# mLSTM: a fixed issue order of state, denominators and h, a shared gate buffer, one store per output block

## The chip, the cores and the metric

The kernel runs on one core of a Trainium2 chip. The engines meant below are TensorE (PE in the profile, its weight loads PEld), VectorE (DVE), ScalarE (ACT), GpSimd (POOL) and SyncE (SP, which issues almost all DMAs of this kernel). Each engine works through its own instructions in a fixed order and waits for the others through semaphores. The metric is the device time of one execution in microseconds; a comparison takes the median of several.

## What is computed

One encoder layer on x of 2048 tokens x 1024 channels. Three token mixers (a bidirectional mLSTM, a neighbourhood attention, a cross-attention into 256 memory tokens) read one normalised input; their outputs are projected, merged by sigmoid gates, projected again, and a squared-ReLU MLP follows. The change touches the mLSTM alone. Cut to one chunk and one direction, it computes:

```
b      = cumsum(lf);  m_t = max(b + m_state, max_s d_log)          # rows, per token and head
s      = (q k^T) * exp(d_log - m_t)                                # causal scores
num    = s v + w_inter * (C q);   den = sum(s) + w_inter * (n q)
h      = num / max(|den|, exp(-m_t))
C_new  = decay * C + sum_s ws * v k^T ;  n_new likewise
...
h_m    = rmsnorm(h_fwd + h_bwd) * sigmoid(o)                       # 4 heads x 128
```

The forward direction goes over the sequence from its start, the backward one from its end.

## The kernel before

Three phases, each with its own PSUM and SBUF pools. Phase 1 computes the input projection block by block (four blocks of 512 tokens) together with the two attentions. Phase 2 runs the mLSTM while TensorE computes merge gates (`late_gates`, L610): dense groups of 24 matmuls, each 128x512, that come from `ch_group`, and that have little to do with the mLSTM. Phase 3 is the merge, the output projection and the MLP. Every dense fp32 product is three matmuls (L234, L235, L236: high x high, high x low, low x high), for which weights are split into a high part (ACT, L178) and a low part (DVE, L179).

**Order.** TensorE's order is the order in which the program is written (`manual_schedule`, L248). On the other engines a scheduler that works ahead of time picks the order from priorities (earlier in the program comes first) and from its own estimate of when each operand is ready; nothing is reordered on the chip.

**Ticks.** `ch_group` calls `tick` after every second k, four times per group, and each call advances `ml_stream` (L640) by one yield. Four ticks are a slot; slots go forward and backward in turn. A chunk (128 tokens, one direction, all four heads) is a generator, `ml_chunk` (L787), that lives for four slots of its direction: ages 0 to 3. The table `when` (L651) says how many steps of which age run in which tick. Tick 3, after the last matmuls of a dense group, holds nearly all of the mLSTM's own matmuls: call it the burst. In each tick the stream also advances `ml_rows` (L740) by one step: the row quantities (cumulative sums and running maxima by `tensor_tensor_scan`, then small transposes) of the next block of four chunks, for both directions. A set of rows has twelve steps; one set is started at slots 3, 11 and 19 each.

**A chunk's steps.** (A) loads: `sk` (scores and k^T that the other direction stored when it came by that chunk, so that the second visit need not compute them; `given`), `qk`, `v1`, `rb`, `wb`. (B) the decay matrix `de` (ACT exp L821, POOL mask L823). (C) transposes of k (PE L833) into a PSUM tile, a copy into `sk` (ACT L835, first visit), `kw` = k weighted (DVE L838), `qw` (POOL L842). (D) scores (PE L853) and `pt` = scores x `de` (DVE L855, or L847 from `sk`), copies into `sk` (ACT L857), its store. (E) load of `hf`, the other direction's h (second visit). (F) numerators and denominators into the pair of PSUM tiles `pn` (PE L869, L872). (G) the state's update (PE L878, DVE L884), the denominators (ACT abs L889, DVE L890, L892), `h` (DVE L895, two instructions, which read `pn`); on a first visit `h` is stored and the chunk ends; on the second `hf` is added (L900), squares are summed (ACT L903), POOL computes the root (L327, L328), and `og`, the output gate, is loaded (L906). (H) `og` x `h` and the normalisation (DVE L909, L910). (I) transposes (PE L914), a high and a low part `hm` (ACT L916, DVE L917) and two stores.

The order of the steps in the burst is `[3, 1, 2, 1, 2, 0]` by age: I, C, F, D, G, A. PSUM in phase 2 has two tiles for the dense groups, two for `pn` (so one chunk's pair at a time) and four called `mx` for all else: k^T takes one, the scores two, the state's update one. `sk`, `og` and `hm` have one SBUF buffer each (`sk` and `og` per direction), `h` two per direction.

Of the kernel before, what the change touches and what calls it, by code (L numbers as in the profile page):

```python
# [3 lines left out]

# [1 line left out]

# [4 lines left out]
F32 = mybir.dt.float32  # L13
F32R = mybir.dt.float32r
BF16 = mybir.dt.bfloat16
AF = mybir.ActivationFunctionType
ALU = mybir.AluOpType
# [6 lines left out]
TB = 512  # L24
# [15 lines left out]
NB = S // TB  # L40
# [42 lines left out]
class Body:  # L83
# [11 lines left out]
    def t(self, tag, shape, bufs, dt=F32):  # L95

        self.n += 1
        return self.p_a.tile(list(shape), dt, name=f"{tag}_{self.n}", tag=tag, bufs=bufs)
# [191 lines left out]
    def scratch(self):  # L290
        d = lambda name, shape, dt=F32: self.p_d.tile(shape, dt, name=name)
        self.scr = dict(
            qk=d("s_qk", [128, 4, S]),
            v=[d(f"s_v{b}", [TB, 512]) for b in range(NB)],
            og=[d(f"s_o{b}", [TB, 512]) for b in range(NB)],
            gate=[d(f"s_g{b}", [24, 128, TB]) for b in range(NB)],
            qs=d("s_qs", [128, 8, 2, 2, 2, 128]),
            ks=d("s_ks", [128, 2, 2, S]),
            vna=d("s_vna", [2, ROWS, 40, 256]),
            hf=[d(f"s_hf{c}", [128, 512]) for c in range(S // 128)],  # L300
            sk=[d(f"s_sk{c}", [128, 6, 128]) for c in range(S // 128)],
            hna=d("s_hna", [128, 2, 2, S]),
            hmem=d("s_hmem", [128, 2, 2, S]),
            ig=d("s_ig", [8, S]),
            fg=d("s_fg", [8, S]),
            lf=d("s_lf", [8, S]),
            w=[[d(f"s_w{i}{b}", [4, TB]) for b in range(NB)] for i in range(2)],
            r=[[d(f"s_r{i}{b}", [4, 4, 128]) for b in range(NB)] for i in range(2)],
            hm=[d(f"s_hm{b}", [128, 2, 4, TB]) for b in range(NB)],
            hT={b: d(f"s_hT{b}", [128, 2, 8, TB]) for b in SPILL},  # L310
            x2=[d(f"s_x2{b}", [TB, D]) for b in range(NB)],

            a=[[d(f"s_a{i}{q}", [128, 3, 2, TB]) for q in range(FF // 512)] for i in range(NB // 2)],
            s=[[d(f"s_s{i}{q}", [128, 4, 2, TB]) for q in range(FF // 512)] for i in range(NB // 2)],
            t=[d(f"s_t{q}", [128, 2, 2, 2, 512]) for q in range(FF // 512)],
        )
# [321 lines left out]
    def ml_stream(self):  # L640


        rows = self.ml_rows(0)
        for tick in range(START_2):
            if tick >= ROWS_2:
                next(rows, None)
            yield
        slot = 0
        dirs = [list(range(16)), list(range(15, -1, -1))]
        live = [[], []]  # L650
        when = {0: [3, 2], 1: [1], 2: [], 3: [3, 1, 2, 1, 2, 0]}  # L651
        d = 0
        while any(dirs) or any(live[0]) or any(live[1]):
            c = dirs[d].pop(0) if dirs[d] else None

            if slot % 8 == 3 and slot < 24:
                rows = self.ml_rows(slot // 8 + 1)
            slot += 1
            live[d] = [None if c is None else self.ml_chunk(d, c)] + live[d][:3]
            for tick in range(4):  # L660
                for age in when[tick]:
                    if age < len(live[d]) and live[d][age]:
                        next(live[d][age], None)
                next(rows, None)
                yield
            if len(live[d]) == 4:
                live[d][3] = None
            d = 1 - d
# [29 lines left out]
    def ml_consts(self):  # L698
        nc, p = self.nc, self.p_a
        t = lambda name, shape, dt=F32: p.tile(shape, dt, name=name)  # L700


        self.reset = t("reset", [36, TB])
        nc.vector.memset(self.reset, 1.0)
        nc.vector.memset(self.reset.rearrange("p (c t) -> p c t", t=128)[:, :, 0:1], 0.0)
        self.carry = t("carry", [36, 1])
        nc.vector.memset(self.carry, NEG)
        self.pack = [t("r_" + x, [36, TB + 2 * (x == "m")]) for x in "ifbmw"]
        for x in self.pack:
            nc.gpsimd.memset(x, 0.0)  # L710
        self.rows = {}
        self.state = [None, None]

    def row(self, tag, shape, bufs=2):
        self.n += 1
# [24 lines left out]
    def ml_rows(self, n):  # L740
# [35 lines left out]
        for d, b, hs in dirs:  # L776
# [7 lines left out]
            nc.vector.tensor_copy(ac, p[:, :, 4:8])  # L784
            self.rows[d, b] = dict(em=em, ac=ac)

    def ml_chunk(self, d, c):  # L787

        nc = self.nc
        b, cc = c // 4, c % 4  # L790
        cs = slice(cc * 128, cc * 128 + 128)
        first = c == (0 if d == 0 else 15)
        final = c == (15 if d == 0 else 0)
        tl = 127 if d == 0 else 0
# [4 lines left out]
        given = second and (d, c) != (0, 8)  # L799
        gives = not second and (d, c) != (1, 8)  # L800
        sk = self.t(f"sk{d}", [128, 6, 128], 1) if given or gives else None
# [17 lines left out]
        de = self.t(f"de{d}", [128, 4, 128], 1)  # L819
# [8 lines left out]
        if given:  # L828
            pk = sk[:, 4:6]
        elif gives or not final:  # L830
            pk = self.ps("mx")[:, 0:256].rearrange("p (a b) -> p a b", b=128)
            for j in range(2):
                nc.tensor.transpose(pk[:, j], qk[:, 2 + j], self.ident)  # L833
            if gives:
                nc.scalar.activation(sk[:, 4:6], pk, AF.Copy)  # L835
        if not final:
            kw = self.row(f"kw{d}", (128, 4, 64), bufs=2)
            nc.vector.tensor_tensor(kw, pk.rearrange("p a (b e) -> p (a b) e", e=64),  # L838
                                    de[:, :, tl:tl + 1].to_broadcast([128, 4, 64]), ALU.mult)
        if not first:  # L840
            qw = self.row(f"qw{d}", (128, 2, 128), bufs=2)
            nc.gpsimd.tensor_tensor(qw, qk[:, 0:2], wb, ALU.mult)  # L842
        yield
        pt = self.t(f"pt{d}", [128, 4, 128], 1)
        par = lambda x, i: x.rearrange("p (a b) t -> p a b t", b=2)[:, :, i]
        if given:
            nc.vector.tensor_tensor(pt, sk[:, 0:4], de, ALU.mult)  # L847
        else:
            psc = [self.ps("mx", (128, 2, 128)) for _ in range(2)]
            for j in range(2):  # L850
                for i in range(2):
                    hp = slice(i * 64, i * 64 + 64)
                    nc.tensor.matmul(psc[i][:, j], qk[hp, 2 + j], qk[hp, j], start=True, stop=True)  # L853
            for i in range(2):
                nc.vector.tensor_tensor(par(pt, i), psc[i], par(de, i), ALU.mult)  # L855
                if gives:
                    nc.scalar.activation(par(sk[:, 0:4], i), psc[i], AF.Copy)  # L857
# [8 lines left out]
        pn = [self.ps("pn", (128, 2, 129)) for _ in range(2)]  # L866
# [7 lines left out]
        if not final:  # L874
# [10 lines left out]
                                                   pu[:, j], ALU.mult, ALU.add)  # L885
            self.state[d] = Cn
        den = self.small(4, "l")
        for j in range(2):
            nc.scalar.activation(den[:, j::2], pn[j][:, :, 128], AF.Abs)  # L889
        nc.vector.tensor_tensor(den, den, R["em"][:, cc], ALU.max)  # L890
        rec = self.small(4, "l")
        nc.vector.reciprocal(rec, den)  # L892
        h = self.t(f"h{d}", [128, 4, 128], 2)
        for j in range(2):
            nc.vector.tensor_tensor(par(h, j), pn[j][:, :, 0:128],  # L895
                                    rec[:, j::2].unsqueeze(2).to_broadcast([128, 2, 128]), ALU.mult)
        if not second:
            self.store(self.scr["hf"][c], h.rearrange("p a b -> p (a b)"))
            return
# [2 lines left out]
        for i in range(4):  # L902
            nc.scalar.activation(hf[:, i], h[:, i], AF.Square, accum_out=ss[:, i:i + 1])  # L903
        rs = self.rstd(ss, 128, "l", 0.5)
        og = self.t(f"og{d}", [128, 512], 1)
        nc.sync.dma_start(og, self.scr["og"][b][cs])  # L906
        yield
        og = og.rearrange("p (a b) -> p a b", b=128)
        nc.vector.tensor_tensor(og, og, h, ALU.mult)  # L909
        nc.vector.tensor_tensor(h, og, rs.unsqueeze(2).to_broadcast([128, 4, 128]), ALU.mult)  # L910
        yield
        p = self.ps("tr", (128, 4, 128))
        for j in range(4):
            nc.tensor.transpose(p[:, j], h[:, j], self.ident)  # L914
        hm = self.t("hm", [128, 2, 4, 128], 1, F32R)
        nc.scalar.activation(hm[:, 0], p, AF.Copy)  # L916
        nc.vector.tensor_tensor(hm[:, 1], p, hm[:, 0].bitcast(F32), ALU.subtract)  # L917
        for l in range(2):
            self.store(self.scr["hm"][b][:, l, :, cs], hm[:, l].bitcast(F32))
        yield  # L920


# [367 lines left out]
    def load_mix(self, b, mix):  # L1290

        ts = slice(b * TB, (b + 1) * TB)
        for k in range(0, 8, 2):
            for l in range(2):
                if k < 4:
                    src = self.scr["hm"][b][:, l, k:k + 2]
                else:
                    src = self.scr["hna" if k < 6 else "hmem"][:, l, :, ts]
                self.nc.sync.dma_start(mix[l][:, k:k + 2].bitcast(F32), src)
# [306 lines left out]
```

## Time and profile before

| | us |
|---|---|
| median of three runs | 2906.34 (2905.22 to 2908.27) |
| the profiled execution | 2895.78 |
| its span, first to last instruction | 2894.1 |
| TensorE busy in the span | 2859.8 |
| VectorE / ScalarE / GpSimd busy | 2006.1 / 1185.9 / 211.9 |
| granted TensorE clock, mean | 0.999 |

The profile is that of one execution. Its page gives busy times and groups of instructions; its trace can be asked for windows of time, for who waited for whom, for the chain of work that ended last and for the instructions in order of time. In a timeline's row stand the start and the duration, then engine, line, operation, what is written and read, the shape and the count, and in brackets how long the engine had been idle before it and what ended that. [...] The mLSTM lies between about 975 and 1275 us of the span.

### The profile page before, as it was taken

Reading aid. Unit: us, or ns where it says so; the run is one execution under the profiler, and the core shown is the slowest. Engines: PE = TensorE matmul, PEld = TensorE weight load, DVE = VectorE, ACT = ScalarE, POOL = GpSimd, SP = SyncE. Lnnn points to the kernel's source line nnn. Section 1 sums busy time; section 2 is a strip of 40 time slices with the busy share of each in tenths; the row PEclk is TensorE's granted clock in tenths of the full one; section 3 lists DMA queues with packets and bytes.
Section 4 is the critical chain, followed back from the end, with each engine's and each line's share of the span. In section 5 each row is a group of like instructions: output and inputs, shape, how many; then the busy total and the mean of one; then the engine's idle time right before and its main releaser. Section 6 shows DMA issues by size and latency. Waiting matters only on the chain.

```text
span 2894.1 us, 41892 instructions
## 1 busy us (share of the span) xinstructions
PE 2859.8 (99%) x15052; PEld 2364.5 (82%) x15052; DVE 2006.1 (69%) x3438; ACT 1185.9 (41%) x2256; POOL 211.9 (7%) x382
## 2 busy tenths in 40 slices
PE   8999999999999999999999999999999999999999
PEld 6878788878888888788888888888888888888887
DVE  6676865477664455647598887666785988885666
ACT  6465654445543443432243334433322433344331
POOL 4121310021000022310000000000000000000000
PEclk9999999999999999999999999999999999999999
DMA  8786778877999888988444446657863444476654
GB/s 278 229 279 194 241 238 251 263 221 223 287 297 298 264 266 269 288 270 274 120 136 159 157 149 232 229 190 227 300 205 114 142 149 160 150 249 202 195 189 160
DMA packets 345408, 632.78 MB, mean 219 GB/s; under 512 B 29712, under 2 KB 151504, under 8 KB 345200
## 3 DMA queue, kind: packets, MB, share of 16 engines
q1 hardware_dynamic: 345200, 630.10, 67.6%
q8 instruction: 119, 1.95, 0.3%
q14 instruction: 89, 0.73, 0.1%
HBM read 453.37 MB, written 176.62 MB: 218 GB/s over the span
## 4 chain that ended last, share of the span: by engine, by line
PE 79%; issue 8%; DVE 5%; DMA 5%; ACT 1%; SPq 1%; POOL 1%; DVEq 0%; POOLq 0%; ACTq 0%
PE mm L234 25%; PE mm L236 24%; PE mm L235 24%; DVE ws L179 1%; PE tr L1088 1%; DMA sk<-s_sk 1%; DMA wr<-in_w_units_dram 1%; PE pn L869 1%; PE mx L1069 1%; PE mm L1369 0%; PE mx L1102 0%; DVE cy L688 0%; ACT ws L178 0%; PE mx L1241 0%; PE tr L1231 0%
## 5 line engine op out<-in xcount | busy, mean ns | idle before, releaser
L234 PE MATMUL mm<-X,ws 128*128 128x512 f32 x896 | 348.9, 389 | 0.0
L236 PE MATMUL mm<-X,ws 128*128 128x512 f32 x896 | 348.6, 389 | 0.0
L235 PE MATMUL mm<-X,ws 128*128 128x512 f32 x896 | 348.6, 389 | 0.0
L179 DVE TENSOR_TENSOR ws<-wr,ws 128x1024 fp32r<-128x1024 f32 (+1 forms) x194 | 240.1, 1244 | 118.9 <-ACT ws L178 117.9
L234 PE MATMUL mm<-hT,ws 128*128 128x512 f32 (+1 forms) x712 | 283.5, 398 | 1.3 <-ACT ev L564 0.7
L236 PE MATMUL mm<-hT,ws 128*128 128x512 f32 (+1 forms) x712 | 277.0, 389 | 0.0
L235 PE MATMUL mm<-hT,ws 128*128 128x512 f32 (+1 forms) x712 | 276.8, 389 | 0.0
L234 PE MATMUL mm<-ws,hT 128*128 128x512 f32 (+2 forms) x704 | 258.4, 367 | 2.6 <-ACT zif L528 1.9
L178 ACT ACTIVATE ws<-wr 128x1024 fp32r<-128x1024 f32 (+1 forms) x194 | 204.1, 1057 | 122.0 <-PE mm L236 87.4
L236 PE MATMUL mm<-ws,hT 128*128 128x512 f32 (+2 forms) x704 | 249.9, 355 | 2.0 <-DVE hT L437 2.0
L235 PE MATMUL mm<-ws,hT 128*128 128x512 f32 (+2 forms) x704 | 248.7, 353 | 0.0
L236 PE MATMUL mm<-X 128*128 128x512 f32 x616 | 239.7, 389 | 0.1
L234 PE MATMUL mm<-X 128*128 128x512 f32 x616 | 239.6, 389 | 0.0
L235 PE MATMUL mm<-X 128*128 128x512 f32 x616 | 239.6, 389 | 0.0
L204 ACT ACTIVATE ws<-wr 128x512 fp32r<-128x512 f32 x224 | 135.0, 628 | 220.4 <-PE mm L236 139.8
L236 PEld LDWEIGHTS mm<-X,ws 128*128 128x128 f32 x896 | 168.2, 188 | 35.0
L235 PEld LDWEIGHTS mm<-X,ws 128*128 128x128 f32 x896 | 168.2, 188 | 34.8
L234 PEld LDWEIGHTS mm<-X,ws 128*128 128x128 f32 x896 | 168.2, 188 | 34.7
L1491 ACT ACTIVATE X<-X 128x1024 fp32r<-128x1024 f32 x109 | 115.5, 1062 | 197.4 <-DMA X<-s_t 58.8
L1492 DVE TENSOR_TENSOR X<-X 128x1024 fp32r<-128x1024 f32 x109 | 132.6, 1223 | 75.6 <-ACT X L1491 75.2
L1518 DVE TENSOR_TENSOR acc<-acc,mm 128x512 f32<-128x512 f32 x192 | 126.1, 683 | 64.1 <-PE mm L236 64.1
L234 PEld LDWEIGHTS mm<-hT,ws 128*128 128x128 f32 x712 | 134.0, 188 | 29.8 <-issue 4.3
(286 smaller groups left out, 5976.7 us busy)
## 6 DMA issues: line engine op xcount, KB each, us to landing
wr<-in_w_units_dram SPq DMA_DIRECT2D x290, 512.0 KB
s_s<-u SPq DMA_DIRECT2D x32, 1024.0 KB
s_g<-ev SPq DMA_DIRECT2D x96, 256.0 KB
ev<-s_g SPq DMA_DIRECT2D x96, 256.0 KB
s_a<-u SPq DMA_DIRECT2D x96, 256.0 KB
X<-s_s SPq DMA_DIRECT2D x45, 512.0 KB
nab<-in_rpb_dram SPq DMA_DIRECT2D x96, 220.0 KB
xt<-in_w_units_dram SPq DMA_DIRECT2D x32, 512.0 KB
```

The costliest lines, as they stand in the source:

```text
L178: nc.scalar.activation(w[:, 0], raw, AF.Copy)
L179: nc.vector.tensor_tensor(w[:, 1], raw, w[:, 0].bitcast(F32), ALU.subtract)
L204: nc.scalar.activation(hi, src, AF.Copy)
L234: mm(out, lhs[0], rhs[0], start=first, stop=False)
L235: mm(out, lhs[0], rhs[1], start=False, stop=False)
L236: mm(out, lhs[1], rhs[0], start=False, stop=last)
L869: mm(pn[h % 2][:, h // 2], pt[:, h], v1[:, h], start=h < 2, stop=first)
L1069: nc.tensor.matmul(psc[:, :nk], q[:, h, u["half"] * 128:u["half"] * 128 + 128], kl, start=True, stop=True)
L1088: nc.tensor.transpose(ptp[0:120, j], sb[:, j * 120:(j + 1) * 120], self.ident)
L1491: nc.scalar.activation(hi, src, AF.Copy)
L1492: nc.vector.tensor_tensor(lo, src, hi.bitcast(F32), ALU.subtract)
L1518: nc.vector.tensor_tensor(c, c, p, ALU.add)
```

## The change

1. `h` of the step before first: `ml_chunk` keeps, for the chunk that just computed its `h`, the last ACT abs (L889) and the last DVE `h` (L895) in `self.marks`. A new context `behind()` gives each instruction traced in it an edge to the mark on its own engine, so that the scheduler issues it later on that engine. It is an order, not a wait: no semaphore is added.
2. Step C is split: the transposes and `qw` stay; `kw` and the copy of k^T move into a new step with `pt` and the other copies. Step D is split into the scores' matmuls and that new step, which is held `behind()`. Step I is split into the transposes and `hm` with its store, `hm` held `behind()`; in H only the second multiplication is.
3. `when` for tick 3 becomes `[3, 1, 2, 1, 2, 3, 1, 0]`: I's transposes, C's transposes, F, D's scores, G, then `hm`, then `kw` and `pt`, then A. TensorE meets its matmuls in the burst in the same order as before.
4. `ml_rows` advances in ticks 0 to 2 only, three steps a slot in place of four.
5. Buffers: `og` three, shared by both directions (before: one each); `h` one per direction (two); `hm` two (one).
6. `hm` is stored by one DMA in place of two; the DRAM scratch `s_hm` has its axes merged, with the same bytes at the same places, and `load_mix` reads it accordingly.

```diff
-            hm=[d(f"s_hm{b}", [128, 2, 4, TB]) for b in range(NB)],
+            hm=[d(f"s_hm{b}", [128, 8, TB]) for b in range(NB)],
...
-        when = {0: [3, 2], 1: [1], 2: [], 3: [3, 1, 2, 1, 2, 0]}
+        when = {0: [3, 2], 1: [1], 2: [], 3: [3, 1, 2, 1, 2, 3, 1, 0]}
...
-                next(rows, None)
+                if tick < 3:
+                    next(rows, None)
...
+    @contextlib.contextmanager
+    def behind(self):
+
+        with contextlib.ExitStack() as stack:
+            for ins in self.marks:
+                stack.enter_context(self.tc.issue_after(ins))
+            yield
...
-            if gives:
-                nc.scalar.activation(sk[:, 4:6], pk, AF.Copy)
-        if not final:
-            kw = self.row(f"kw{d}", (128, 4, 64), bufs=2)
-            nc.vector.tensor_tensor(kw, pk.rearrange("p a (b e) -> p (a b) e", e=64),
-                                    de[:, :, tl:tl + 1].to_broadcast([128, 4, 64]), ALU.mult)
...
-        if given:
-            nc.vector.tensor_tensor(pt, sk[:, 0:4], de, ALU.mult)
-        else:
+        if not given:
...
-            for i in range(2):
+        yield
+        with self.behind():
+            if gives:
+                nc.scalar.activation(sk[:, 4:6], pk, AF.Copy)
+            if not final:
+                kw = self.row(f"kw{d}", (128, 4, 64), bufs=2)
+                nc.vector.tensor_tensor(kw, pk.rearrange("p a (b e) -> p (a b) e", e=64),
+                                        de[:, :, tl:tl + 1].to_broadcast([128, 4, 64]), ALU.mult)
+            if given:
+                nc.vector.tensor_tensor(pt, sk[:, 0:4], de, ALU.mult)
+            for i in range(2) if not given else ():
                 nc.vector.tensor_tensor(par(pt, i), psc[i], par(de, i), ALU.mult)
                 if gives:
                     nc.scalar.activation(par(sk[:, 0:4], i), psc[i], AF.Copy)
...
-            nc.scalar.activation(den[:, j::2], pn[j][:, :, 128], AF.Abs)
+            marks.append(nc.scalar.activation(den[:, j::2], pn[j][:, :, 128], AF.Abs))
...
-        h = self.t(f"h{d}", [128, 4, 128], 2)
+        h = self.t(f"h{d}", [128, 4, 128], 1)
...
+        self.marks = marks[1].ins, marks[3].ins
...
-        og = self.t(f"og{d}", [128, 512], 1)
+        og = self.t("og", [128, 512], 3)
...
-        nc.vector.tensor_tensor(h, og, rs.unsqueeze(2).to_broadcast([128, 4, 128]), ALU.mult)
+        with self.behind():
+            nc.vector.tensor_tensor(h, og, rs.unsqueeze(2).to_broadcast([128, 4, 128]), ALU.mult)
...
-        hm = self.t("hm", [128, 2, 4, 128], 1, F32R)
-        nc.scalar.activation(hm[:, 0], p, AF.Copy)
-        nc.vector.tensor_tensor(hm[:, 1], p, hm[:, 0].bitcast(F32), ALU.subtract)
-        for l in range(2):
-            self.store(self.scr["hm"][b][:, l, :, cs], hm[:, l].bitcast(F32))
+        yield
+        hm = self.t("hm", [128, 2, 4, 128], 2, F32R)
+        with self.behind():
+            nc.scalar.activation(hm[:, 0], p, AF.Copy)
+            nc.vector.tensor_tensor(hm[:, 1], p, hm[:, 0].bitcast(F32), ALU.subtract)
+        self.store(self.scr["hm"][b][:, :, cs], hm.rearrange("p l h t -> p (l h) t").bitcast(F32))
...
-                    src = self.scr["hm"][b][:, l, k:k + 2]
+                    src = self.scr["hm"][b][:, 4 * l + k:4 * l + k + 2]
```

More of the change, by code (lines that the diff above doesn't have):

```diff
@@ L7 @@
+import contextlib
 import functools
@@ L712, in ml_consts @@
         self.state = [None, None]
+        self.marks = ()
     def row(self, tag, shape, bufs=2):
@@ L887, in ml_chunk @@
         den = self.small(4, "l")
+        marks = []
         for j in range(2):
-            nc.scalar.activation(den[:, j::2], pn[j][:, :, 128], AF.Abs)
+            marks.append(nc.scalar.activation(den[:, j::2], pn[j][:, :, 128], AF.Abs))
         nc.vector.tensor_tensor(den, den, R["em"][:, cc], ALU.max)
@@ L892, in ml_chunk @@
         nc.vector.reciprocal(rec, den)
-        h = self.t(f"h{d}", [128, 4, 128], 2)
+        h = self.t(f"h{d}", [128, 4, 128], 1)
         for j in range(2):
-            nc.vector.tensor_tensor(par(h, j), pn[j][:, :, 0:128],
-                                    rec[:, j::2].unsqueeze(2).to_broadcast([128, 2, 128]), ALU.mult)
+            marks.append(nc.vector.tensor_tensor(par(h, j), pn[j][:, :, 0:128],
+                                                 rec[:, j::2].unsqueeze(2).to_broadcast([128, 2, 128]), ALU.mult))
+        self.marks = marks[1].ins, marks[3].ins
         if not second:
```

## The prediction

> **What bounds the kernel now.** I read the page's engine table first, then the windows over the mLSTM's stretch, then TensorE's waits, then the instructions in order of time around each of them.
>
> ```profile
> span 2894.1 us, 41892 instructions
> PE 2859.8 (99%) x15052; PEld 2364.5 (82%) x15052; DVE 2006.1 (69%) x3438; ACT 1185.9 (41%) x2256; POOL 211.9 (7%) x382
> 975.00:1115.00 140.00, 137.45 (x912) 112.88 (x911) 75.67 (x179) 58.32 (x176) 28.59 (x47) 1.00 0.85 265
> 1115.00:1275.00 160.00, 157.95 (x978) 129.69 (x977) 101.65 (x211) 70.20 (x270) 42.92 (x75) 1.00 0.88 270
> PE pn L869 <- DVE h L895: 2.6, 2, 1.5
> PE pn L869 <- ACT de L821: 2.0, 3, 1.1
> ```
>
> The first two rows are the page's, the next two the windows that hold the whole mLSTM (length, then the busy time of PE, PEld, DVE, ACT, POOL, then clock and DMA), the last two from the list of waits (total, times, longest). TensorE sets the time. In the 300 us that the change touches it is idle for 140.00 - 137.45 = 2.55 us and 160.00 - 157.95 = 2.05 us: 4.60 us together, 0.16% of the run. And all of it stands in one place: 2.6 + 2.0 us ahead of L869, the first matmuls into `pn`. That is the most that the change can win by removing idle time. The rest of TensorE's work in the stretch keeps its number, its order and, at a granted clock of 1.00, its speed.
>
> Now two of the five waits, on TensorE and then on VectorE.
>
> ```profile
> 1054.04 0.38 PE L833 MATMUL mx<-ident,qk 128*128 128x128 f32 x2
> 1055.94 1.13 PE L869 MATMUL pn<-v,pt 128*128 128x129 f32 x8 [1.52 <-DVE h L895]
> ...
> 1220.19 1.02 PE L869 MATMUL pn<-v,pt 128*128 128x129 f32 x7 [1.11 <-ACT de L821]
> ```
>
> ```profile
> 1047.32 1.21 DVE L754 TENSOR_TENSOR_SCAN r_b<-reset,r_f 4x512 f32<-4x512 f32 x1 [5.66 <-DMA r_f<-s_lf]
> 1048.46 1.25 DVE L760 TENSOR_TENSOR_SCAN r_m<-r_f,r_m,r_i 4x512 f32<-4x512 f32 x1
> 1049.64 1.19 DVE L179 TENSOR_TENSOR ws<-wr,ws 128x1024 fp32r<-128x1024 f32 x1
> 1050.75 0.40 DVE L838 TENSOR_TENSOR kw<-mx,de 128x256 f32<-128x256 f32 x1
> 1051.09 0.73 DVE L855 TENSOR_TENSOR pt<-mx,de 128x256 f32<-128x256 f32 x2
> ...
> 1052.44 1.22 DVE L754 TENSOR_TENSOR_SCAN r_b<-reset,r_f 4x512 f32<-4x512 f32 x1
> ...
> 1055.26 0.76 DVE L895 TENSOR_TENSOR h<-pn,sm 128x256 f32<-128x256 f32 x2
> ...
> 1056.20 0.68 DVE L763 TENSOR_TENSOR r_i<-r_i,r_b 36x512 f32<-36x512 f32 x1
> ...
> 1057.63 1.81 DVE L771 TENSOR_TENSOR r_w<-r_b,r_m 4x512 f32<-4x512 f32 x2
> ```
>
> There is one pair of `pn` tiles, so a burst's L869 waits for the `h` of the burst before. Here that `h` ends at 1055.26 + 0.76 = 1056.02, just when L869 starts. Ahead of it VectorE had waited for the row loads until 1047.32, then done two scans, a weight split, `kw`, `pt`, the state and more row work, another scan among it.
>
> ```profile
> 1216.48 0.43 DVE L838 TENSOR_TENSOR kw<-sk,de 128x256 f32<-128x256 f32 x1 [4.05 <-DMA sk<-s_sk]
> 1216.82 0.69 DVE L910 TENSOR_TENSOR h<-og,rs 128x512 f32<-128x512 f32 x1
> ...
> 1218.03 0.80 DVE L847 TENSOR_TENSOR pt<-sk,de 128x512 f32<-128x512 f32 x1
> ...
> 1219.52 0.74 DVE L895 TENSOR_TENSOR h<-pn,sm 128x256 f32<-128x256 f32 x2
> 1218.98 0.64 SPq L803 DMA_DIRECT2D sk<-s_sk  x1
> ```
>
> The longest of the three waits named after `de` is the same wait: `h` ends at 1219.52 + 0.74 = 1220.26, where L869 starts at 1220.19. VectorE stood 4.05 us at a `kw` whose `sk` had not landed, with that `h` behind it. It is a loop: `sk` has one buffer per direction, its next load is issued (SP, last row, 1218.98) when `pt` (to 1218.83) has read it, and the `kw` that waits for such a load stands in VectorE's queue about a slot before its turn in the program, ahead of the `h` of an earlier burst. Of a slot of 8.49 us (below) 4.05 are lost there.
>
> **The change part by part.**
>
> *`h` ahead of `kw`, `pt`, `hm`.* In the second half (three waits, 2.0 us) `kw` can no longer stand ahead of its slot's `h`, so the 4.05 us of waiting for `sk` fall behind it, and the load has two slots to land. I take these 2.0 us as gone. In the first half (two waits, 1.52 us and the rest of 2.6, about 1.0) what leaves the place ahead of `h` is `kw` and `pt`, 0.40 + 0.73 = 1.13 us. The scans and the weight split, on which no edge is put, may stay there. So the shorter wait goes wholly and 1.52 falls to 0.39: 1.0 + 1.13 = 2.1 us gone. Bounds: nothing gained (the scheduler fills the place with another split of 1.19 us) and 2.6 us (the scans move too). I take 2.1, since in the quoted slot `kw` and `pt` are 1.13 of the delay by measurement.
>
> What is late next? Behind `h` now wait `kw` and `pt` for two slots hence, which nobody needs soon, and the PSUM tiles that they read. For that I need a slot's shape.
>
> ```profile
> 1082.63 0.38 PE L833 MATMUL mx<-ident,qk 128*128 128x128 f32 x2
> ...
> 1084.39 0.61 PE L853 MATMUL mx<-qk 64*128 64x128 f32 x8
> ...
> 1085.52 0.50 PE L234 MATMUL mm<-hT,ws 128*128 128x512 f32 x1
> ...
> 1091.12 0.38 PE L833 MATMUL mx<-ident,qk 128*128 128x128 f32 x2
> 1067.22 0.43 PE mm L234
> 1068.68 0.76 DVE L895 TENSOR_TENSOR h<-pn,sm 128x256 f32<-128x256 f32 x2
> 1040.52 0.72 ACT L857 ACTIVATE sk<-mx 128x256 f32<-128x256 f32 x2 [1.29 <-DVE pt L855]
> ```
>
> A burst takes 1085.52 - 1082.63 = 2.89 us, then 5.60 us of dense matmuls follow, and the scores begin 1.76 us into the next burst. A first-half burst takes all four `mx` tiles. The state's is read first and serves the next k^T; the scores' two must be free 5.60 + 1.76 = 7.36 us after the burst. In a slot without row work `h` ends 1068.68 + 0.76 - 1067.22 = 2.22 us after its burst; `kw`, `pt` and half of the last row's copies add 0.40 + 0.73 + 0.36, which makes 3.7 us. 3.6 us of room: cost nothing. ACT's copies wait behind the abs and for `pt`; the dense groups' evacuation behind them has a slot of 8.49 us, so nothing there either.
>
> [...]
>
> *Rows in ticks 0 to 2.* No work goes; a set of twelve steps takes four slots, not three, and is done at the set's fourth slot, two slots before its first user is loaded. TensorE's transposes for the second direction leave the burst for the middle of a dense group.
>
> ```profile
> 1071.15 0.39 PE L236 MATMUL mm<-hT,ws 128*128 128x512 f32 x1
> 1071.47 0.22 PE L781 MATMUL mx<-ident,r_m 4*128 4x4 f32 x1
> ...
> 1072.40 0.40 PE L235 MATMUL mm<-hT,ws 128*128 128x512 f32 x1
> ...
> 1076.47 0.22 PE L781 MATMUL mx<-ident,r_m 4*128 4x4 f32 x1
> ...
> 1077.05 0.50 PE L234 MATMUL mm<-hB,ws 128*128 128x512 f32 x1
> ```
>
> Behind a burst they cost 1077.05 - 1076.47 = 0.58 us. Inside a group, from L236 to L235, 1072.40 - 1071.15 = 1.25 us, where two dense matmuls alone would take 0.46: 0.79 us. That is 0.21 us more, three times: +0.6 us. They need an `mx` tile half a dense stretch, 2.8 us, after the burst, when at least the state's is free; bound 0 to 1 us, I take 0.
>
> *Buffers and stores.*
>
> ```profile
> ACT hm L916 <- DMA s_hm<-hm: 4.6, 4, 1.7
> 1190.81 0.38 SPq L104 DMA_DIRECT2D s_hm<-hm  x1
> SPq L104 <- ACT sk L857: 19.2, 14, 3.9
> 1094.12 5.38 DMA s_g<-ev
> ```
>
> The second `hm` ends four waits of ACT, none of them on TensorE's path: nothing. One store fewer for each of 16 blocks is 16 x 0.38 = 6 us of SP, on which TensorE waits nowhere in this stretch: nothing. One `h` per direction: the first-half `h` must be stored before its direction's next, 17 us later, and a store of this size lands in about 5.4 us (last row, a store of the same 256 KB): nothing; it would cost if SP fell 10 us behind. SP already waits for ACT's copies at the store of `sk` (19.2 us in 14 times); these now come behind `h` and `pt`, about 1 us later, and behind that store stand the loads of the next chunk and of weights. TensorE waits for none of them here, and the chunk's loads have a slot to spare: nothing, against about 1 us in each of 15 slots if that cover went. Three shared `og`: a load comes a slot sooner; nothing.
>
> *Sum*: -2.0 - 2.1 + 0.6 = -3.5 us. On the profiled span 2894.1 becomes 2890.6. The profiled execution took 2895.78 us, 10.6 less than the median of 2906.34; as the change acts on counted microseconds, I take the same 3.5 us from the median: **2902.8 us**, 0.12% down. About 0.2% (5.8 us) is what a measurement of this kernel can tell from no change, so I expect no difference that can be told.
>
> **The rivals.**
>
> *First-half waits stay.* The row scans remain ahead of `h` and a weight split fills the place of `kw` and `pt`. For: splits and scans carry no edge. Against: with `kw` gone, 1.13 us are gone too unless something takes their place. -2.0 + 0.6: 2904.9.
>
> *The change doesn't do what it says.* If the edges only move the wait (the `og` product, which has no edge, waits for its load ahead of `h` as `kw` did for `sk`), the idle time stays and the switching is paid: 2906.9. Against: `og` is loaded more than a slot ahead of its product.
>
> *Slower: the score tiles come free late.* In the row slot above `h` ended at 1056.02; its burst had ended a dense stretch of 5.60 us before 1054.04, so 7.6 us earlier; without `kw` and `pt` it is 6.5. If then `r_i`, `r_b`, `r_w` (1056.20 to 1059.44, 3.2 us) run before `kw` and `pt`, the score tiles are free at 6.5 + 3.2 + 1.5 = 11.2 us, against the 7.36 that decide: TensorE waits 3.8 us at L853. Three sets give +11.4; with the forecast's -3.5 that is +7.9: 2914.2. Against: `kw` and `pt` come earlier in the program than those rows, so that the scheduler prefers them once `h` is issued.
>
> *Faster.*
>
> ```profile
> PE mm L234 <- ACT ev L607: 1.4, 2, 0.7
> ```
>
> All five waits go (4.6), the switching costs nothing, and the waits for ACT's evacuations near the stretch go too (1.4 us by the same list): -6.0, 2900.3.
>
> **How the numbers follow.** Forecast 0.55; first-half waits stay 0.15; no effect 0.07; slower 0.14; faster 0.09. Forecast, first and second rival lie within 0.2%: 0.77, of which I give 0.02 to each side for what the trace cannot show of the scheduler's choices. Faster 0.11, within 0.73, slower 0.16. The range holds forecast and the first two rivals and reaches halfway into the others, whose sizes are bounds: 2899 to 2913.
>
> **What would show it.** Right: no idle before L869 between 975 and 1275 us, or one of 0.4 us in a row slot; `kw` and `pt` behind `h` on VectorE; the 4 us before `kw` on `sk` no longer ahead of `h`; the second direction's small transposes 0.2 us dearer. Wrong: idle time of TensorE before L853 or L833 (score tiles), before L781, or before L234 (evacuations), or a stretch outside phase 2 that moved.

## The result, and the profile after

| | before, us | changed, us |
|---|---|---|
| median of nine runs each on one chip | 2905.22 (2901.48 to 2910.51) | 2894.83 (2890.84 to 2899.52) |
| ratio, 95% interval | | 0.9965 (0.9954 to 0.9976) |
| the profiled execution's span | 2894.1 | 2893.1 |

The change takes 10.4 us off, 0.36%, where the prediction had 3.5 us and "no difference that can be told"; the time lies 4.2 us below the lower end of its range. The first two lines of the changed kernel's page:

```profile
span 2893.1 us, 41875 instructions
PE 2861.0 (99%) x15052; PEld 2364.8 (82%) x15052; DVE 2004.3 (69%) x3438; ACT 1187.3 (41%) x2256; POOL 216.4 (7%) x382
```

The two profiled spans differ by 1.0 us only, while the medians differ by 10.4. So the pair of spans says nothing of the change; where the time went must be read inside the stretch. The windows of the changed kernel over the mLSTM (length, busy time of PE, PEld, DVE, ACT, POOL, clock, DMA share, GB/s):

```profile
975.00:1115.00 140.00, 140.00 (x923) 114.80 (x922) 75.71 (x170) 58.11 (x173) 27.17 (x47) 1.00 0.83 262
1115.00:1275.00 160.00, 160.00 (x989) 131.75 (x988) 99.79 (x220) 73.15 (x277) 47.06 (x77) 1.00 0.88 279
```

TensorE is busy for 140.00 of 140.00 and 160.00 of 160.00 us. The 4.60 us of idle time are gone, all five waits. And VectorE's order of time in the changed kernel, one slot of the second half:

```profile
1205.52 0.58 DVE L897 SCALAR_TENSOR_TENSOR C<-C,wb,mx 128x129 f32<-128x129 f32 x2
1206.02 0.74 DVE L909 TENSOR_TENSOR h<-pn,sm 128x256 f32<-128x256 f32 x2
...
1207.88 0.42 DVE L863 TENSOR_TENSOR kw<-sk,de 128x256 f32<-128x256 f32 x1
1208.21 0.68 DVE L866 TENSOR_TENSOR pt<-sk,de 128x512 f32<-128x512 f32 x1
...
1216.34 0.68 DVE L866 TENSOR_TENSOR pt<-sk,de 128x512 f32<-128x512 f32 x1
```

`kw` and `pt` stand behind `h`, and no bracket stands behind `kw`: it waits for nothing. From one `pt` to the next are 1216.34 - 1208.21 = 8.13 us, TensorE's own pace of about 8.2 us a slot.

The same line before tells what the prediction overlooked. VectorE's `pt` in the kernel before, the first and the last of four in a row:

```profile
1189.71 0.67 DVE L847 TENSOR_TENSOR pt<-sk,de 128x512 f32<-128x512 f32 x1
...
1218.03 0.80 DVE L847 TENSOR_TENSOR pt<-sk,de 128x512 f32<-128x512 f32 x1
```

That is (1218.03 - 1189.71)/3 = 9.44 us a turn. `pt` frees `sk`, the load is issued, `kw` waits for it, and the rest of VectorE's work stands behind `kw` until the next `pt`: the loop of the prediction, but with a period of its own, in these turns some 1.2 us longer than TensorE's slot. Not every turn is that long: from the first `pt` that reads `sk` to the fifteenth, over the 14 turns of the second half, the mean is 8.70 us (1127.38 to 1249.12), against 8.34 us in the changed kernel (1131.89 to 1248.67). A turn that is longer than the slot takes the difference from the lead that VectorE has over TensorE, and TensorE waits only when the lead is used up: here at 1201.40, 1210.61 and 1220.19, at the end of the row of long turns. What one execution shows as idle time is what is left after the lead.

### The profile page after: what moved, and what is told of

Same layout as the page of the kernel before. It is cut to its first block, busy times and chain, and to the rows that moved or that the text cites. A ratio compares the mean times of both kernels' runs of the same rounds, so it can differ in the third digit from the quotient of the medians.

```text
span 2893.1 us, 41875 instructions
## 1 busy us (share of the span) xinstructions
PE 2861.0 (99%) x15052; PEld 2364.8 (82%) x15052; DVE 2004.3 (69%) x3438; ACT 1187.3 (41%) x2256; POOL 216.4 (7%) x382
## 4 chain that ended last, share of the span: by engine, by line
PE 89%; DVE 3%; issue 3%; DMA 3%; ACT 1%; POOL 0%; SPq 0%; DVEq 0%; POOLq 0%; ACTq 0%
PE mm L235 27%; PE mm L237 27%; PE mm L236 27%; PE tr L1105 1%; PE pn L882 1%; PE mx L1086 1%; PE mx L1119 1%; PE pn L885 1%; PE mx L891 1%; DVE ws L180 1%; DMA nav<-s_vna 1%; PE mx L1258 1%; PE tr L1248 1%; DMA xt<-in_xT_dram 0%; DMA wr<-in_w_units_dram 0%
```

## The experiments

Theory A, throughout: the gain is that loop (one `sk` buffer, `kw` on VectorE ahead of `h`), and its price varies with the lead. In the first twelve expectations the other letters stand for rivals that are spelled out there; from the thirteenth on, B, C, C1 and C2 are new theories, of another question. Ratios are to the kernel before, in runs on the same chip.

**1. The kernel before once more** (no edit).

> The kernel before, unchanged, to see an execution of usual length: the one in the profile took 2895.8 us, the median is 2905.2. Theory A (the loop over sk): a transfer that lands later is paid one for one, so the missing 9 us stand before L869 between 975 and 1290 us: 10 us or more of TensorE idle there, most of it after 1130 us. Theory B (row work): the same sum, but between 1040 and 1115 us, at the row sets. Theory D (elsewhere): idle before L869 stays near 4.6 us and the 9 us stand in phase 1 or in the tail. Times: ratio 1.00 for all.

2903.47 us, ratio 0.9988 (0.9978 to 0.9998): two sets of runs of one program differ by 0.1%, just beyond the stated interval, which is the size of error to keep in mind below. Its profile is another execution. TensorE's waits in the stretch, in the first half (first row) and the second (second row):

```profile
PE pn L869 <- DVE h L895: 4.1, 2, 2.5
PE pn L869 <- ACT de L821: 5.6, 6, 1.6
```

These are 9.7 us in eight waits, where the first profile had 4.6 in five, of the same program. VectorE's order of time over a turn, and two loads of `sk` as SP issues them (`SPq` is SP's queue):

```profile
1192.34 0.68 DVE L847 TENSOR_TENSOR pt<-sk,de 128x512 f32<-128x512 f32 x1
...
1194.64 1.00 DVE L900 TENSOR_TENSOR h<-h,hf 128x512 f32<-128x512 f32 x1
1195.68 0.69 DVE L909 TENSOR_TENSOR og<-og,h 128x512 f32<-128x512 f32 x1
1200.64 0.43 DVE L838 TENSOR_TENSOR kw<-sk,de 128x256 f32<-128x256 f32 x1 [4.27 <-DMA sk<-s_sk]
1200.98 0.68 DVE L910 TENSOR_TENSOR h<-og,rs 128x512 f32<-128x512 f32 x1
...
1203.56 0.75 DVE L895 TENSOR_TENSOR h<-pn,sm 128x256 f32<-128x256 f32 x2
```

```profile
1194.42 1.13 SPq L803 DMA_DIRECT2D sk<-s_sk  x1
...
1213.21 0.82 SPq L803 DMA_DIRECT2D sk<-s_sk  x1
```

`pt` ends at 1193.02, the load is issued at 1194.42, `kw` starts at 1200.64, and the `h` of the burst comes 2.92 us behind it. Now the length of the stretch, by the first and the last of the matmuls into `pn` (duration min/median/max in ns, then first and last start), for the kernel before, this run and the changed kernel:

```profile
L869 PE MATMUL pn<-v,pt x256: 271/275/348, 994.3 to 1261.9; 128*128 128x129 f32 x128
```

```profile
L869 PE MATMUL pn<-v,pt x256: 271/275/349, 991.8 to 1265.2; 128*128 128x129 f32 x128
```

```profile
L882 PE MATMUL pn<-v,pt x256: 272/275/277, 998.3 to 1260.6; 128*128 128x129 f32 x128
```

267.6, 273.4 and 262.3 us. Against the first profile the change is worth 5.3 us, against the second 11.1, and the medians say 10.4. Run 4 below, a kernel without the edges that takes as long as the one before, gives a third pair, in which both profiles are of the execution with the median time (2906.65 and 2894.83 us):

```profile
L869 PE MATMUL pn<-v,pt x256: 271/275/552, 997.4 to 1271.6; 128*128 128x129 f32 x128
```

274.2 - 262.3 = 11.9 us, where the two times differ by 11.8. In this pair the whole difference lies inside the stretch. So the execution in which the prediction counted was a short one of its kernel (its 2895.78 us lie below all nine times of before, 2901.48 to 2910.51), and short in this very place.

**2 to 4. One part alone**: the edges with the split of the steps (parts 1 to 3 of the change), the rows in three ticks (part 4), the buffers and the single store (parts 5 and 6), each in the kernel before.

```diff
+        self.marks = marks[1].ins, marks[3].ins
...
+        with self.behind():
```
```diff
-                next(rows, None)
+                if tick < 3:
+                    next(rows, None)
```
```diff
-        h = self.t(f"h{d}", [128, 4, 128], 2)
+        h = self.t(f"h{d}", [128, 4, 128], 1)
...
-        og = self.t(f"og{d}", [128, 512], 1)
+        og = self.t("og", [128, 512], 3)
...
```

> Only the split steps, their order and the edges behind abs and h; rows in all four ticks, buffers and the two stores as before. Theory A: nearly all of the gain, 9 us (ratio 0.997), no idle before L869 after 1130 us. Theory B: 2 to 3 us, since row scans still stand ahead of h in four ticks. Theory C (buffers): 2 us at most, since one og and one hm hold up SP. Theory D: anything within 3 us.

> Only the rows kept off tick 3. Theory A: within 2 us of before; the wait for sk ahead of h stays. Theory B: 7 us or more faster. Theory C and D: within 2 us.

> Only the buffers (og three shared, h one, hm two) and one store of hm. Theory A and B: within 2 us of before. Theory C (SP held up at the og load and the hm stores lets sk's load go late): 7 us or more faster, with kw waiting less than 2 us for sk.

| | us | ratio, 95% interval |
|---|---|---|
| edges alone | 2898.14 | 0.9975 (0.9965 to 0.9985) |
| rows alone | 2903.83 | 0.9998 (0.9989 to 1.0008) |
| buffers and store alone | 2906.65 | 1.0004 (0.9994 to 1.0014) |

The edges, together with the split of the steps, carry most of the gain; the other two are nothing by themselves. With the edges alone no wait before `pn` is left, but a new one has come, in the first half:

```profile
PE mx L783 <- DVE kw L862: 2.1, 2, 1.4
```

L783 are the row work's small transposes. Their tile among the four `mx` is the one that `kw` reads, and `kw` now stands behind `h`. In TensorE's order of time with the edges alone:

```profile
1073.61 0.66 PE L890 MATMUL mx<-v,kw 128*64 128x129 f32 x8
1075.63 0.19 PE L783 MATMUL mx<-ident,r_m 4*128 4x4 f32 x1 [1.36 <-DVE kw L862]
```

Rows in tick 3 put these transposes right behind the burst, where `kw` has just been held back. This is the slower rival's mechanism (what stands behind `h` frees its PSUM late), met by other matmuls than the rival's, and at 2.1 us instead of 11.4 (it is not in the changed kernel, whose rows stay out of tick 3).

**5 and 6. The loop broken without the edges, and the split without the edges.** Five is the kernel before with two `sk` buffers per direction (and one `h`, to make room); six is the changed kernel without its marks, so that `behind()` gives no edge.

```diff
-        sk = self.t(f"sk{d}", [128, 6, 128], 1) if given or gives else None
+        sk = self.t(f"sk{d}", [128, 6, 128], 2) if given or gives else None
...
-        h = self.t(f"h{d}", [128, 4, 128], 2)
+        h = self.t(f"h{d}", [128, 4, 128], 1)
```
```diff
-        self.marks = marks[1].ins, marks[3].ins
```

> The kernel before with two sk buffers per direction (h one per direction, to make room), no edges. Theory A (the loop pt, load of sk, kw through one sk buffer, with kw ahead of h): the load is issued two slots ahead, so no wait of kw for sk over 1 us after 1150 us and no idle before L869 in the second half; the first-half waits stay (2.5 to 4 us): 5 to 7 us faster, ratio about 0.998. Rival A' (VectorE's sheer load ahead of h, not the load of sk): the second-half waits stay, ratio 1.000.

> The kernel after without its edges: split steps, their order, rows in ticks 0 to 2 and all buffers stay. If the edges do it (theory A): kw stands ahead of h again, idle before L869 of 4 us or more, ratio 0.9985 to 1.000. If the order in which the steps are written is enough (rival): ratio 0.9965, as the kernel after.

Five: 2896.05 us, ratio 0.9974 (0.9963 to 0.9985). The second half has no wait before `pn` left; in the first half are 1.5 us before `pn` and 0.9 before the row transposes. VectorE in run 5:

```profile
1188.54 0.68 DVE L847 TENSOR_TENSOR pt<-sk,de 128x512 f32<-128x512 f32 x1
...
1198.58 0.43 DVE L838 TENSOR_TENSOR kw<-sk,de 128x256 f32<-128x256 f32 x1
...
1205.06 0.68 DVE L847 TENSOR_TENSOR pt<-sk,de 128x512 f32<-128x512 f32 x1
```

`kw` waits for nothing, though it still stands ahead of an `h`, and two turns of `pt` take 1205.06 - 1188.54 = 16.52 us, 8.26 each. One buffer more does for the second half what the edges do, with `kw` still early. That is the strongest evidence for theory A: the loop is what was cut, by either means. The gaps of 4.05 us (first profile, before 1216.48) and 4.27 us (run 1, before 1200.64) stand on VectorE, though TensorE is the engine that sets the pace; that they came from too few buffers, run 5 shows.

Six: 2897.26 us, ratio 0.9979 (0.9968 to 0.9990), between what the two expectations had, with 5.2 us of idle time before `pn` in its profile. The order in which the steps are written doesn't move `kw` by itself: it still stands ahead of `h`, and waits.

```profile
1206.90 0.42 DVE L863 TENSOR_TENSOR kw<-sk,de 128x256 f32<-128x256 f32 x1 [1.82 <-DMA sk<-s_sk]
...
1211.51 0.76 DVE L909 TENSOR_TENSOR h<-pn,sm 128x256 f32<-128x256 f32 x2
```

The list of VectorE's waits in the second half of run 6:

```profile
DVE kw L863 <- DMA sk<-s_sk: 22.0, 7, 8.6
```

In the kernel before the same list has 31.5 us in 11 waits. So the split, the rows and the buffers without the edges bring some 6 us of the 10, with the loop still there; which of them does it no run shows, and neither is it shown what the edges would bring without the split.

**9 and 10. Two parts together**: edges and rows with the old buffers and two stores; edges and buffers with the rows in all four ticks.

> Edges and rows in ticks 0 to 2, with the buffers and the two stores of before. If the buffers and the single store are worth nothing: as the kernel after, 9 to 10 us faster than before (ratio 0.9965 to 0.997), with no idle before L869 nor before the rows' small transposes. If they matter once the edges are there (rival: SP's queue is the next limit, since e8 lost 19 us to five more issues a slot): 0.998 or above, with idle before the transposes of h.

> Edges and buffers, rows in all four ticks. If the rows' move only removes the 2.1 us that the edges alone showed before the rows' small transposes (they wait there for kw to free its PSUM tile) and costs 0.6 us: 1.5 us slower than the kernel after, ratio 0.997 to 0.9975, with about 2 us of idle before those transposes. If the move does more (row scans ahead of h): 4 us or more slower than the kernel after.

Nine: 2894.06 us, ratio 0.9960 (0.9948 to 0.9973), which is the whole change's. Ten: 2898.10, ratio 0.9973 (0.9962 to 0.9984), with the same 2.1 us before L783 as the edges alone. So the gain is some 7 us of the edges with the split and another 3 to 4 us for keeping the rows off tick 3 (4.0 us between runs 9 and 10, on one chip), which by itself is worth nothing: it removes a wait that only the edges bring. By the traces that second part is 2.1 us; the rest can't be told from the error of the runs. Buffers and store add nothing that can be measured.

**7, 8, 11, 12. A load of `sk` meant to land later**, in the kernel before and in the changed one: cut into six loads (7, 8), or read in pieces of 256 bytes from a padded scratch (11, 12).

```diff
-            nc.sync.dma_start(sk, self.scr["sk"][c])
+            for j in range(6):
+                nc.sync.dma_start(sk[:, j], self.scr["sk"][c][:, j])
```
```diff
-            sk=[d(f"s_sk{c}", [128, 6, 128]) for c in range(S // 128)],
+            sk=[d(f"s_sk{c}", [128, 12, 80]) for c in range(S // 128)],
...
```

> The kernel before with the load of sk as six DMAs in place of one (same bytes), so that it lands later by five issues of SP, 2 to 3 us. Theory A: the loop runs once a slot on 11 to 13 slots and each turn grows by that: 15 to 30 us slower, all of it before L869 in the second half. Rival A' or D: within 4 us.

> The kernel after with the same six DMAs. Theory A: the load has two slots to land, nothing before L869; as the kernel after, ratio 0.9965 to 0.998. Rival (the load of sk still sets the pace, or SP's issue time does): slower than the kernel after by 10 us or more.

> [...] Theory A (the loop through sk): 5 to 25 us slower, in step with how much later kw starts after the issue, all before L869 in the second half. Rival (only SP's issue time counts): within 3 us of before.

> The kernel after with the same short pieces. Theory A: the load has two slots, so nothing before L882 (pn) in the second half; as the kernel after, ratio 0.9965 to 0.998. Rival: as much slower than the kernel after as e11 is than before.

| | before, us | changed, us |
|---|---|---|
| six loads | 2918.85, 1.0054 (1.0038 to 1.0070) | 2914.16, 1.0043 (1.0028 to 1.0058) |
| pieces of 256 bytes | 2910.84, 1.0016 (1.0007 to 1.0025) | 2927.98, 1.0081 (1.0067 to 1.0095) |

A miss. The changed kernel, in which the load of `sk` has 15 us from issue to `kw`, was to take a slower one for nothing; it lost 19 and 33 us (counted from 0.9965 of the kernel before on the same chip), more than the kernel before (14 and 5). The kernel before lost its time elsewhere than expected, too: mainly at the transposes of `h` (9.6 us with six loads, 10.0 us with short pieces), not before `pn`. TensorE waits there (L931) in the changed kernel with six loads as well:

```profile
DVE h L916 <- DMA hf<-s_hf: 24.4, 9, 4.7
PE tr L931 <- DVE h L927: 16.3, 6, 5.3
```

It is not `sk` that is late, but `hf`, which was not touched.

**13 and 14. Is it `hf` held behind the load of `sk`?** The changed kernel with six loads, and `hf` issued by ScalarE; and edges and rows with six loads and two `sk` buffers.

```diff
-            nc.sync.dma_start(hf, self.scr["hf"][c].rearrange("t (h e) -> t h e", h=4))
+            nc.scalar.dma_start(hf, self.scr["hf"][c].rearrange("t (h e) -> t h e", h=4))
```

> The changed kernel with the load of sk cut into six (as in the run of that name, 2914.16 us), and the load of hf issued by ScalarE instead of SP. Theory B (in the changed kernel the load of hf stands behind the waiting load of sk in SP's queue, the sum h + hf waits for it, and kw and pt stand behind that sum): hf no longer waits for pt, so the waits at h + hf for hf and TensorE's waits at the transposes of h go, and the time falls to 2894 to 2902 us. Theory C (six transfers are dear in themselves, by SP's issue time and the slower landing, whatever stands behind them): the time stays at 2910 to 2916 us.

> The edges and the shifted row work with the buffers of before, the load of sk cut into six, and two sk buffers per direction (one h buffer, to make room). Theory B: the load of sk no longer waits for the pt of the slot before, so nothing is held behind it in SP's queue; TensorE's waits at the transposes go, 2894 to 2902 us. Theory C: SP issues as many transfers as before and each sk lands as late after its issue, so 2910 to 2916 us.

2914.48 (1.0043, 1.0029 to 1.0058) and 2917.22 us (1.0048, 1.0033 to 1.0063). Theory B falls: the loss stayed in both (22 and 25 us, counted in the same way). In 14 VectorE still waits 22.2 us for `hf`. In 13, with `hf` off SP, the wait for it went, as B said, but `og`, the next load in SP's queue, was late in its place:

```profile
DVE og L925 <- DMA og<-s_o: 18.1, 4, 6.7
PE tr L931 <- DVE h L927: 11.3, 5, 4.4
```

**15 and 16. SP's time or the landing of `sk`?** Eight loads of 4 rows of 32 bytes, which nothing reads, behind the one load of `sk`, in the changed kernel and in the one before.

```diff
+            for j in range(8):
+                nc.sync.dma_start(self.t("few", [4, 8], 24), self.scr["qk"][0:4, j % 4, c * 128:c * 128 + 8])
```

> The changed kernel with its one load of sk as it was, and eight loads of 4 rows of 32 bytes behind it on SP, which nothing reads. A small load of SP's takes 0.36 us (r_f from s_lf, 4x512, in the trace of the changed kernel), so SP gets some 2.9 us a slot more to issue, as with five more loads of 64 KB at 0.6 us, while hardly a byte more is moved and sk lands as before. Theory C1 (what cost 19 us is SP's issue time: 0.62 of the stretch plus 2.9 of a slot of 8.25 us is 0.97, so SP falls behind and hf, og and wb are late): 2908 to 2918 us, with waits of TensorE at the transposes of h. Theory C2 (what cost it is the later landing of sk itself): 2893 to 2898 us, no such waits.

> The kernel before with the same eight small loads behind each load of sk. Theory C1: 2910 to 2920 us, waits at the transposes of h, as with sk cut into six (2918.85 us). Theory C2: 2902 to 2908 us, no waits at the transposes.

2942.02 us (1.0139, 1.0124 to 1.0154) and 2935.79 us (1.0113, 1.0096 to 1.0130). No sign of C2, and a loss beyond C1's ranges: some 50 us in the changed kernel (counted as above) and 34 in the one before, for loads that together move 1 KB a chunk. One turn of SP in the changed kernel with the small loads, in order of time (start, duration):

```profile
1209.01 0.67 SPq L814 DMA_DIRECT2D sk<-s_sk  x1
1209.73 5.38 SPq L816 DMA_DIRECT2D few<-s_qk  x8
1215.21 0.39 SPq L819 DMA_DIRECT2D qk<-s_qk  x1
...
1216.96 1.25 SPq L830 DMA_DIRECT2D wb<-s_w  x2
1218.25 0.59 SPq L105 DMA_DIRECT2D s_g<-ev  x1
...
1219.37 0.45 SPq L878 DMA_DIRECT2D hf<-s_hf  x1
1219.86 0.48 SPq L923 DMA_DIRECT2D og<-s_o  x1
1220.44 0.57 SPq L105 DMA_DIRECT2D s_hm<-hm  x1
1221.11 0.81 SPq L814 DMA_DIRECT2D sk<-s_sk  x1
```

A turn of SP takes 1221.11 - 1209.01 = 12.10 us, against TensorE's 8.2, and between the rows stand no more than 0.1 us. But the row of eight runs from the start of the first small load to the end of the last. What one of them took SP (ns, least, median and most of 120), and what SP waited for between them, from 1209 to 1216 us:

```profile
L816 SPq DMA_DIRECT2D few<-s_qk x120: 239/293/1152, 1081.6 to 1281.6; - x120
SPq L816 <- DMA s_hm<-hm: 1.0, 1, 1.0
SPq L816 <- DMA sk<-s_sk: 0.7, 1, 0.7
```

So a small load took 0.29 us at the median, less than the 0.36 us of the expectation, and 1.7 of the 5.38 us are not issuing: SP stood at a small load until a store and a load that it had issued earlier had landed. From 1155 to 1275 us such waits at the small loads add up to 24.8 us; in the changed kernel SP waits for no transfer in that window. Why a load that touches neither tile waits for them isn't shown. Without the 1.7 us the turn would still be 10.4 us, more than TensorE's 8.2. So SP's queue sets the pace, by the time to issue and by these waits together; the runs don't part the two. TensorE waits for it at the transposes:

```profile
PE tr L932 <- DVE h L928: 32.4, 10, 6.2
```

The DMA engines are less busy meanwhile. The hardware queue from 1155 to 1235 us, packets, MB and share of 16 engines, in the changed kernel and then with the small loads:

```profile
q1 hardware_dynamic: 26004, 25.05, 97.7%
```

```profile
q1 hardware_dynamic: 18611, 17.26, 69.9%
```

In the changed kernel itself their packets take nearly all of the time (97.7%); with the small loads more than a quarter of that is free again, and the kernel is slower.

So these runs were no test of theory A. With six loads SP's turn is 12 us too (from 1202.51 to 1214.58 in run 8, with waits for landings in it as well), and with short pieces the load next behind `sk` stays on SP for long; the changed kernel with pieces of 256 bytes, SP in order of time:

```profile
1199.69 0.68 SPq L814 DMA_DIRECT2D sk<-s_sk  x1
1200.46 5.10 SPq L817 DMA_DIRECT2D qk<-s_qk  x1
...
1210.50 0.67 SPq L814 DMA_DIRECT2D sk<-s_sk  x1
```

10.8 us a turn. Why that issue takes 5.10 us instead of 0.4 to 0.6 was not tried apart, and no row shows whether `sk` itself landed later with short pieces; in the kernel before with short pieces the scheduler's order on VectorE differed as well (`kw` at 1204.11, right ahead of its `pt` at 1204.45). Theory A rests on runs 1, 2, 5 and the turns of `pt`, and covers the second half. The waits before `pn` in the first half, where no `kw` reads a loaded `sk`, are the other part of the gain: 2.6, 4.1, 2.4 and 4.6 us in the kernel before, in run 1, 3 and 4, none in run 2. What they stand behind is the prediction's reading (`kw`, `pt` and row work ahead of `h`); no run took that apart.

## Why the prediction was wrong

**The step that failed** is the term of the sum for the second half: "three waits, 2.0 us ... I take these 2.0 us as gone", and with it the sentence that carried the count over, "as the change acts on counted microseconds, I take the same 3.5 us from the median". The mechanism was the one that acted: `sk`'s one buffer, its load, `kw` ahead of `h`, one slot a turn. Only its size was read from the idle time of one execution. The same program showed 5.6 us there in its next profile. Before `pn`, in both halves together, the four profiles of kernels without the edges that are no faster than the one before have 4.6 (the prediction's), 9.7 (run 1), 4.2 (run 3) and 8.9 us (run 4, the execution with the median time). The prediction had both signs in hand: 2895.78 us against a median of 2906.34, and the loop itself, described, but with no turn measured. The turns say how far VectorE falls behind: 8.70 us against a slot of 8.25, 14 times, is an estimated 6 us in the first profile, and 9.02 us (1126.38 to 1252.70) in run 1's 11 us. TensorE paid 2.0 and 5.6 us of that; the lead covered the rest. Why one execution starts the second half with more lead than another stays open: the profiles end phase 1 at different times (first `pn` from 991.8 to 998.3 us) without a pattern.

**First half, -2.1**: "1.52 falls to 0.39" was too careful, and the count came from the same short execution. The waits before `pn` went altogether, and they were 2.6 us in the first profile, 4.1 in run 1 and 4.6 in run 4.

**The row transposes, +0.6**: paid as forecast. In the changed kernel the second direction's take as long as the first's, 0.90 to 0.91 us from the start of the dense matmul ahead to the start of the one behind, and bring no idle time. (In the kernel before, dense matmuls of 128x512 are recorded with 0.39 to 0.40 us each but start 0.23 us apart, from 1086.09 to 1090.89 us.) But "They need an `mx` tile half a dense stretch, 2.8 us, after the burst ... I take 0" had a second side: with the rows left in tick 3 the edges cost 2.1 us there. The rows' part was not only a price: it makes the edges worth their full gain.

**"3.6 us of room: cost nothing"** for the score tiles held: no run with the edges waited at the scores for a PSUM tile of `kw` or `pt`, and the slower rival's 3.8 us in each row slot did not come.

**Buffers and one store, "nothing"**: right (runs 4 and 9). The reason given, that TensorE waits nowhere for SP, holds only while SP's turn fits into TensorE's slot of 8.2 us: with five and with eight loads more a chunk it took 12 us (runs 8 and 15).

**The rivals**: "Faster" named the right event, all five waits gone, but its 2900.3 was built from the same short execution. "First-half waits stay" and "the change doesn't do what it says" are refuted by the windows above.

**The price of the edges**, the slower rival's kind of wait, was paid where they came without the rows' move (runs 2 and 10), at the row transposes instead of the scores: TensorE waited 2.1 us there for the `kw` that stood behind `h`.

## What to carry to other kernels

Where a buffer's free, load and use form a loop through an engine's queue, measure its turn (from one use to the next) and set it against the slot of the engine that should set the pace; the idle time in one profile shows only what is left after the lead (2.0 us of an estimated 6 here), and a profiled execution that is shorter than all timed runs can understate it, as here. A second buffer and a later place in the queue cut the same loop here (ratios 0.9974 and 0.9975, runs 5 and 2), so price both. After holding work back behind an edge, look at who needs the PSUM tiles that it reads, and before adding transfers, add up the time that one queue needs to issue a slot's worth of them, and look for what that queue itself waits for.

## What the runs showed of the hardware

*SP's queue set the pace in run 15*, with a turn of 12.10 us against TensorE's 8.2. A load of 128 bytes took SP 0.24 to 1.15 us to issue, 0.29 at the median (run 15); the load of `sk`, 384 KB, took 0.32 us in the changed kernel (at 1208.92) and 0.67 in run 15 (at 1209.01). Eight small loads a chunk cost some 50 us of the kernel's time, in part by waits of SP for the landing of earlier transfers (24.8 us at the small loads from 1155 to 1275 us), while the share of the DMA engines fell from 97.7 to 69.9% (1155 to 1235 us). In the turn of run 15 shown above SP's rows follow each other within 0.1 us; 1.7 us of waiting stand inside the row of small loads. Runs 11 and 12, with pieces of 256 bytes, lost 5 and 33 us, but what in them did it was not taken apart.

*VectorE beside GpSimd.* VectorE's product of `og` and `rs` (L910) took 0.68 us at 1200.98 in run 1, but 1.23 us in the same run where GpSimd had begun to multiply `qw` just before:

```profile
1189.45 1.23 DVE L910 TENSOR_TENSOR h<-og,rs 128x512 f32<-128x512 f32 x1 [0.19 <-POOL rs L328]
```

```profile
1189.39 0.74 POOL L842 TENSOR_TENSOR qw<-qk,wb 128x256 f32<-128x256 f32 x1
```

That is 0.55 us on VectorE, inside the loop that set the price here. Where VectorE began first, at 1161.42 in the first profile, its product took 0.68 us and the `qw` beside it (1161.61) 1.09, where the median of the 30 `qw` in that profile is 0.76. That either slowed the other isn't shown: no run took `qw` away.
